# Decode scores of a half batch in three runs of two, two and one feature stages instead of two runs of three and two

## The chip, the core and the metric

The kernel runs on one core of one Trainium2 chip. The engines that matter here are TensorE (PE in the profile; its weight loads are listed as PEld), VectorE (DVE), ScalarE (ACT) and GpSimd (POOL), which issues the indirect DMAs that gather cache pages. The metric is the device time of one execution in microseconds, as the median of several runs.

## What is computed

The reference is one inference step of one layer, for a prompt of 512 tokens and for a decode batch of 8 sequences with 4 new tokens each. Both groups share the weights.

```python
def layer(h, pos, past_ckv, past_kr, past_pos, s0, lb, norm_g, wg, wu, wd, ...):
    h = h + 0.5 * rmsnorm(swiglu(rmsnorm(h, norm_g[0]), wg[0], wu[0], wd[0]), norm_g[1])
    m, c_kv, k_r, s_fin = mixer(rmsnorm(h, norm_g[2]), pos, past_ckv, past_kr, past_pos, s0, lb, ...)
    h = h + rmsnorm(m, norm_g[3])
    h = h + 0.5 * rmsnorm(swiglu(rmsnorm(h, norm_g[4]), wg[1], wu[1], wd[1]), norm_g[5])
```

The part that the change touches is the decode attention inside `mixer`. For each sequence, 16 queries (4 tokens times 4 heads) attend to 4096 past positions. A past position has a latent row of 256 numbers and a rotary key of 64 numbers, both found through a page table:

```python
s = (jnp.einsum('bqhr,bsr->bhqs', ql, c_kv) + jnp.einsum('bqhd,bsd->bhqs', qr, k_rope)).astype(jnp.float32) * scale
p = jax.nn.softmax(s, axis=-1).astype(c_kv.dtype)
return jnp.einsum('bhqs,bsr->bqhr', p, c_kv)
```

## The kernel before, in words

**The stretch of the program.** After the attention of the prompt the kernel enters a scope called `dec`. There two generators are advanced in turn: `decode()` does the decode attention, and `gb` is the second feed-forward block for the first half of the tokens (256 columns). Each call of `next` on `decode()` is one step; after it `gb` is advanced about once. `gb` is the generator `ffn` with `fine=True`; its matrix multiplications are recorded on lines L259, L277 and L288, with weights split into a high and a low part on ScalarE (L250, `wh`) and VectorE (L251, `wl`).

**Halves.** The past of each of the 8 sequences is cut in two halves of 2048 positions, so there are 16 objects `Half`. Each half goes through these parts:

- `gather` fetches two blocks of latent rows (`craw`, 1 MB each, L1352) and `gather_r` two blocks of rotary keys (`rraw`, L1359), as indirect DMAs that GpSimd issues. A `craw` block sits in one of seven slots (`ulb`, `uhb`, `ha`, `hb`, `mb`, `q0`, `dx`; the profile prints `q0` as `q`). `rraw` has two buffers, so the next `gather_r` waits until VectorE has transposed the current one.
- `turn(st)` transposes 64 of the 320 features of the half (two instructions of 128x512 on VectorE, L1367) into a tile `kh`. There are five such feature stages; stage 0 holds the rotary keys, stages 1 to 4 the latent. `kh` has four buffers (`KHB = 4`), so a fifth `turn` waits until the scores have read the first.
- `score(st)` multiplies a stage's `kh` by the queries: 16 fp32 products of 64 rows by 32 columns over 128 positions, on L1379. The profile counts each of them as two MATMULs with a weight load each, so a stage is 32 MATMULs and a half is 160. The last stage copies the scores out of PSUM (L1385) and takes a maximum (L1387, `mxh`).
- `peak` turns the scores into probabilities: one small product `pm` (L1391), a maximum (L1393), the exponential (L1397), a transpose to `pt` (L1399) and 16 small copies into `pbuf` (L1403), 12 of them on ScalarE and 4 on VectorE.
- `value` multiplies the probabilities by `craw` (32 MATMULs for the two blocks, L1412). When a block has been read, the next `craw` gather may go into its slot. `gathered` (L1420, L1421) collects a sequence once both halves are done.

**What sets the order.** `decode()` runs over `n` and, within it, over five steps `st`. In each step it first scores the stages that the table `RUNS` names for this step, for half `n - 2`; then it may run `peak` (step 1) and `value` (step 4) for half `n - 3`; then it makes one `turn`. So the scores of one half are two bursts of MATMULs within a sequence of feed-forward matrix products: stages 0, 1, 2 in step 2 and stages 3, 4 in step 4, the second directly ahead of `value`. The layer that records the instructions may still move an instruction ahead of others of its engine where its inputs are there.

```python
RUNS = {2: (0, 1, 2), 4: (3, 4)}
```

Of the kernel before, what the change touches and what calls it, by code (L numbers as in the profile page):

```python
# [64 lines left out]
JS = ((8, 9), (0, 1), (2, 3), (4, 5), (6, 7))  # L65
KHB = 4
PEAK = 1
RUNS = {2: (0, 1, 2), 4: (3, 4)}
LEVELS = (32, 16, 8, 4, 2, 1)
CH = 64  # L70

# [39 lines left out]
def hybrid_step_kernel(  # L111
# [443 lines left out]
    with scope("ffn0") as pool:  # L555
# [143 lines left out]
        if True:  # L699
            if True:  # L700
                sst.close()
                st = stg.enter_context(tc.tile_pool(name="st", bufs=1, side="right", reuse_waits="tile"))
# [585 lines left out]
    with scope("dec"):  # L1288
# [134 lines left out]
        def decode():  # L1423
            H = [Half(n) for n in range(NH2)]
            blocks = [h_ for h_ in H for _ in range(2)]
            ups = [(h_, st) for h_ in H for st in range(len(JS))]

            def gather(n=1):
                for h_ in blocks[:n]:
                    h_.gather()  # L1430
                del blocks[:n]

            def turn():
                if ups:
                    h_, st = ups.pop(0)
                    h_.turn(st)
                    if st == 0 and h_.n + 1 < NH2:
                        H[h_.n + 1].gather_r()

            for n in range(NH2 + 4):  # L1440

                def at(k):
                    return H[n - k] if 0 <= n - k < NH2 else None

                for st in range(len(JS)):
                    if at(2):
                        for k in RUNS.get(st, ()):
                            at(2).score(k)
                    if n < 3 and st == 0:
                        if n == 0:  # L1450
                            H[0].gather_r()
                        gather(2 + n // 2)
                    if st == PEAK and at(3):
                        at(3).peak()
                    if st == 1 and at(4) and at(4).i:
                        at(4).gathered()
                    if st == len(JS) - 1 and at(3):
                        for c in range(2):
                            at(3).value(at(4), c)
                            gather()  # L1460
                    if n > 1 or n == 1 and st >= 1:
                        if n != 2 or st >= 2:
                            turn()
                    yield

        def decode_end():
# [33 lines left out]
            nc.vector.tensor_copy(oT[1][:, NH:, HS[1] - TS :], o[:, :P].rearrange("p (h t) -> p h t", h=NH))  # L1500

        ga, gn = decode(), decode_new()
        na, ib = len(JS) * (NH2 + 2) + 4, 0
        for ia in range(na):
# [190 lines left out]
```

## Time and profile before

| | us |
|---|---|
| median of 3 runs | 1250.42 (1248.77 to 1251.25) |
| profiled execution | 1257.12 |
| its span, first to last instruction | 1255.3 |
| PE busy | 1225.7 (98%) |
| DVE busy | 983.8 (78%) |
| ACT busy | 742.0 (59%) |
| POOL busy | 72.4 (6%) |

The decode scores (L1379) run from 716.2 to 953.2 us of the span. The granted TensorE clock is 0.995 over the span. A row of a timeline gives the start in us, the duration in us, the engine, the line, the operation with its output and inputs, the count of merged instructions, and in brackets the idle time ahead of it with what ended it ("issue": the engine waited for nothing that the profile shows). A row of stretches gives the stretch, its length, and the busy time of PE, PEld, DVE, ACT and POOL with instruction counts, then the granted clock, the DMA share and GB/s.

### The profile page before, as it was taken

What the parts mean: (1) busy time and instruction counts of PE and PEld (TensorE: products, weight loads), DVE (VectorE), ACT (ScalarE), POOL (GpSimd) and SP (SyncE); (2) the same over time, 40 slices, a digit from 0 to 9 for tenths busy, and PEclk for the clock granted to TensorE, in tenths of its full rate; (3) what the DMA queues carried; (4) which work ended last, traced back from release to release, by engine and by line L of the source; (5) the groups of instructions that cost most, each with busy time, mean ns of one, the idle gap of its engine ahead of it and who ended that gap; (6) DMA issues with size and microseconds to landing.
All of it is one profiled execution on the core that took longest, in us unless ns stands there. A gap on an engine that the chain in (4) does not pass through costs nothing.

```text
span 1255.3 us, 30001 instructions
## 1 busy us (share of the span) xinstructions
PE 1225.7 (98%) x12366; PEld 1157.1 (92%) x12366; DVE 983.8 (78%) x1976; ACT 742.0 (59%) x1559; POOL 72.4 (6%) x80
## 2 busy tenths in 40 slices
PE   8999999999999999999999899999999999999997
PEld 7999999999999988988889889878888999999997
DVE  7897788878679887877876899989987878466665
ACT  7675545544466655446668656665656777554454
POOL 0000000000000000000000412222310000000000
PEclk9999999999999999999999899999999999999999
DMA  6232333322164122324223959778776635645551
GB/s 236 85 118 87 100 101 101 94 96 94 51 227 158 60 89 69 104 77 148 75 92 118 374 178 347 292 249 299 252 273 218 204 104 191 188 137 182 145 160 59
DMA packets 73113, 195.59 MB, mean 156 GB/s; under 512 B 12336, under 2 KB 27728, under 8 KB 68240
## 3 DMA queue, kind: packets, MB, share of 16 engines
q1 hardware_dynamic: 64512, 150.47, 37.0%
q0 software_dynamic: 7168, 41.95, 9.2%
q8 instruction: 97, 1.59, 0.5%
q10 hardware_dynamic: 1296, 1.26, 0.3%
q14 instruction: 40, 0.33, 0.1%
HBM read 183.97 MB, written 9.67 MB: 154 GB/s over the span
## 4 chain that ended last, share of the span: by engine, by line
PE 86%; ACT 6%; DVE 5%; issue 2%; DMA 1%; SPq 0%; DVEq 0%; ACTq 0%
PE acc L259 29%; PE acc L277 18%; PE dn L259 8%; PE Y L561 6%; PE X L561 4%; PE Z L561 4%; PE s L1379 3%; PE acc L717 3%; PE o L1412 2%; ACT wh L250 1%; DVE wl L251 1%; PE pa L938 1%; ACT pbuf L1403 1%; PE acc L288 1%; PE zx L826 1%
## 5 line engine op out<-in xcount | busy, mean ns | idle before, releaser
L250 ACT CAST wh<-wraw 128x1024 fp32r<-128x1024 f32 (+2 forms) x194 | 185.3, 959 | 169.3 <-PE acc L259 108.6
L251 DVE TENSOR_TENSOR wl<-wraw,wh 128x1024 fp32r<-128x1024 f32 (+2 forms) x194 | 214.3, 1107 | 68.6 <-ACT wh L250 67.5
L277 PE MATMUL acc<-uha,wh 128*128 128x256 f32 (+1 forms) x528 | 155.7, 296 | 0.8 <-ACT uha L207 0.8
L277 PE MATMUL acc<-uha,wl 128*128 128x256 f32 (+1 forms) x528 | 150.6, 286 | 0.5 <-DVE wl L251 0.4
L277 PE MATMUL acc<-ula,wh 128*128 128x256 f32 (+1 forms) x528 | 150.9, 286 | 0.0
L259 PE MATMUL acc<-uhb,wh 128*128 128x288 f32 (+1 forms) x432 | 128.0, 296 | 0.0
L259 PE MATMUL acc<-uhb,wl 128*128 128x288 f32 (+1 forms) x432 | 127.0, 295 | 0.9 <-DVE wl L251 0.7
L259 PE MATMUL acc<-ulb,wh 128*128 128x288 f32 (+1 forms) x432 | 127.5, 295 | 0.0
L277 PEld LDWEIGHTS acc<-uha,wh 128*128 128x128 f32 x528 | 99.6, 189 | 8.8 <-issue 7.3
L277 PEld LDWEIGHTS acc<-uha,wl 128*128 128x128 f32 x528 | 99.5, 189 | 2.4 <-DVE wl L251 1.4
L277 PEld LDWEIGHTS acc<-ula,wh 128*128 128x128 f32 x528 | 99.8, 189 | 1.5 <-issue 1.2
L259 PEld LDWEIGHTS acc<-uhb,wl 128*128 128x128 f32 x432 | 81.2, 188 | 1.5 <-DVE wl L251 1.5
L259 PEld LDWEIGHTS acc<-uhb,wh 128*128 128x128 f32 x432 | 81.0, 188 | 0.2 <-ACT uhb L170 0.2
L259 PEld LDWEIGHTS acc<-ulb,wh 128*128 128x128 f32 x432 | 81.1, 188 | 0.1
L259 PE MATMUL dn<-hh,dh 128*128 128x272 f32 x256 | 74.3, 290 | 0.0
L259 PE MATMUL dn<-hh,dl 128*128 128x272 f32 x256 | 73.8, 288 | 0.0
L259 PE MATMUL dn<-hl,dh 128*128 128x272 f32 x256 | 73.6, 287 | 0.0
L1379 PE MATMUL s<-kh,q 64*32 64x128 f32 x2560 | 53.5, 273 | 5.3 <-issue 5.3
L277 PE MATMUL acc<-uhb,wh 128*128 128x272 f32 x176 | 52.8, 300 | 0.0
L1379 PEld LDWEIGHTS s<-kh,q 64*32 64x32 f32 x2560 | 38.5, 105 | 15.4 <-issue 10.5
L259 PE MATMUL acc<-hlb,wh 128*128 128x288 f32 x176 | 52.1, 298 | 0.0
L259 PE MATMUL acc<-hhb,wh 128*128 128x288 f32 x176 | 51.8, 298 | 0.0
(632 smaller groups left out, 3899.0 us busy)
## 6 DMA issues: line engine op xcount, KB each, us to landing
wraw<-w_u SPq DMA_DIRECT2D x66, 512.0 KB
wraw<-w_g SPq DMA_DIRECT2D x65, 512.0 KB
wraw<-w_d SPq DMA_DIRECT2D x40, 384.0 KB
wraw<-w_in SPq DMA_DIRECT2D x24, 512.0 KB
wraw<-w_d SPq DMA_DIRECT2D x32, 320.0 KB
wraw<-w_d SPq DMA_DIRECT2D x16, 512.0 KB
wraw<-w_o SPq DMA_DIRECT2D x16, 512.0 KB
g_S<-state SPq DMA_DIRECT2D x4, 512.0 KB
```

Source lines behind the costliest of these rows:

```text
L250: nc.scalar.copy(wh[:, :kt], w[:, :kt])
L251: nc.vector.tensor_tensor(wl[:, :kt], w[:, :kt], f32(wh[:, :kt]), op=ALU.subtract)
L259: nc.tensor.matmul(out, a, b, start=n == 0, stop=n == last)
L277: nc.tensor.matmul(acc[:, :n], a[:, k], b[:, k], start=k + i == 0, stop=k == kt - 1 and i == 2)
L288: nc.tensor.matmul(acc, a[:, k], b[:, k], start=k + i == 0, stop=k == kt - 1 and i == 2)
L561: nc.tensor.matmul(bank, a[p][:, k], b[q][:, k], start=first and k + n == 0, stop=k == 3 and n == 2, skip_group_check=True)
L717: nc.tensor.matmul(accs[x, d], wts[d][p][:, k], hs[k // 2][q][:, k % 2, x], start=k + n == 0, stop=k == nf - 1 and n == 2)
L826: nc.tensor.matmul(z, w[a][:, k], U[1][b][:, k], start=k + n == 0, stop=k == KD - 1 and n == 2)
L938: nc.tensor.matmul(po[es, c].rearrange("p (n m) -> p n m", m=m), kx[:, cs], up(qx[:, cs], m), start=True, stop=True, skip_group_check=True)
L1379: nc.tensor.matmul(self.s[r][c * 32 : c * 32 + 32, :P], q[rs, j], kh, start=st + jj == 0, stop=st == len(JS) - 1 and jj == 1, skip_group_c ...
L1403: (nc.scalar.copy if g else nc.vector.tensor_copy)(self.p[g * 32 : g * 32 + 32, c // 2, c % 2 * 4 : c % 2 * 4 + 4, self.i * 16 : self.i * ...
L1412: nc.tensor.matmul(o[g : g + 32, :R], self.p[:, c, a], self.craw[c][:, a], start=i + c == 0 and a < 4, stop=i + c == 2 and a >= 4, skip_gr ...
```

## The change

The table that says which stages are scored in which step has three entries instead of two, the first already in step 0, and the transposes of the first two halves are no longer held back for two steps at `n == 2`, so that they are there for the earlier scores. From then on each `turn` belongs to a step that lies two steps earlier against the half's own scores.

```diff
-RUNS = {2: (0, 1, 2), 4: (3, 4)}
+RUNS = {0: (0, 1), 2: (2, 3), 4: (4,)}
@@ decode(), the end of each step
                     if n > 1 or n == 1 and st >= 1:
-                        if n != 2 or st >= 2:
-                            turn()
+                        turn()
                     yield
```

No instruction is added or taken away; they stand in another order. On TensorE, in the half that follows the value product on `ulb` and `uhb` (L288 and L259 are feed-forward products, `s<-kh` the scores, `o<-` the value products; a row counts products, of which the profile shows each score product as two MATMULs; the line with @@ stands for rows that did not change):

```order
 L288 MATMUL acc<-hla,wh 128x256
 L288 MATMUL acc<-hha,wl 128x256
-L1379 MATMUL s<-kh,q_8159 32x128 x32
+L1379 MATMUL s<-kh,q_8159 32x128 x16
 L1412 MATMUL o<-ha,pbuf 32x256 x8
 L1412 MATMUL o<-hb,pbuf 32x256 x8
@@ -5182,4 +5185,5 @@
 L259 MATMUL acc<-hla,wh 128x256
 L259 MATMUL acc<-hha,wl 128x256
+L1379 MATMUL s<-kh,q_8159 32x128 x32
 L259 MATMUL acc<-hha,wh 128x256
 L259 MATMUL acc<-hla,wh 128x256
```

Ahead of the value products there are now 16 score products instead of 32, and a run of 32 stands in the feed-forward products behind them; the run in the middle goes from 48 to 32. Over the whole program the scores stood in 37 unbroken rows and now stand in 52.

On VectorE, behind the split of a feed-forward activation (L171) that the trace of before has at 826.10 us. Before (`pm` and `pt` belong to `peak`, `kh<-rraw` is the transpose of the rotary keys that the next `gather_r` waits for):

```order
L171 TENSOR_TENSOR hla<-sil,hha 128x256
L1393 TENSOR_REDUCE q_8159<-pm 128x16
L1421 COPY q_8787<-o 128x4x16
L1396 SCALAR_TENSOR_TENSOR mq,mbd<-q_8159 128x16
L350 TENSOR_TENSOR sil<-acc,rna 128x256
L1399 STREAM_TRANSPOSE pt<-q_8159 128x256
L1403 COPY pbuf<-pt 32x4x16 x4
L1367 STREAM_TRANSPOSE kh<-ulb 128x512
L1367 STREAM_TRANSPOSE kh<-uhb 128x512
L1367 STREAM_TRANSPOSE kh<-rraw 128x512 x2
```

And with the change:

```order
L171 TENSOR_TENSOR hla<-sil,hha 128x256
L1367 STREAM_TRANSPOSE kh<-ulb 128x512
L1367 STREAM_TRANSPOSE kh<-uhb 128x512
L1367 STREAM_TRANSPOSE kh<-rraw 128x512
L1393 TENSOR_REDUCE q_8159<-pm 128x16
L1421 COPY q_8787<-o 128x4x16
L1396 SCALAR_TENSOR_TENSOR mq,mbd<-q_8159 128x16
L1367 STREAM_TRANSPOSE kh<-rraw 128x512
L1399 STREAM_TRANSPOSE pt<-q_8159 128x256
L350 TENSOR_TENSOR sil<-acc,rna 128x256
L1403 COPY pbuf<-pt 32x4x16 x4
```

The transposes of the last stage and of the rotary keys have moved ahead of the chain of `peak`; the small operations of `peak` and the copies into `pbuf` stand behind them.

## The prediction, made before the changed kernel ran

> **What bounds the kernel now.** The page's first part was read first, then the table of stretches, one stretch for each half, and last the order in time of the engines within a half.
>
> ```profile
> span 1255.3 us, 30001 instructions
> PE 1225.7 (98%) x12366; PEld 1157.1 (92%) x12366; DVE 983.8 (78%) x1976; ACT 742.0 (59%) x1559; POOL 72.4 (6%) x80
> ```
>
> TensorE is busy 98% of the span, so what it does sets the end, and the change moves only TensorE and VectorE work between 711 and 966 us. Below are stretches from the end of one value product to the end of the next, that is one half each (the first row: fourteen halves together).
>
> ```profile
> 748.15:955.37 207.22, 201.26 (x3753) 173.76 (x3753) 187.23 (x412) 125.91 (x335) 47.71 (x49) 1.00 0.79 279
> ...
> 748.15:761.76 13.61, 13.61 (x267) 12.02 (x267) 12.91 (x30) 9.02 (x25) 2.91 (x4) 1.00 0.89 314
> 761.76:777.95 16.19, 16.19 (x289) 14.60 (x289) 15.30 (x30) 10.67 (x28) 4.69 (x6) 1.00 0.95 347
> 777.95:792.28 14.33, 14.33 (x273) 12.73 (x273) 11.96 (x28) 8.53 (x23) 3.35 (x5) 1.00 0.87 328
> 792.28:807.43 15.15, 13.96 (x259) 11.40 (x259) 14.36 (x32) 9.71 (x26) 4.90 (x5) 1.00 0.72 262
> 807.43:821.64 14.21, 13.32 (x255) 10.95 (x255) 13.73 (x33) 8.71 (x25) 4.22 (x5) 1.00 0.81 281
> 821.64:836.44 14.80, 14.50 (x271) 12.63 (x271) 12.06 (x29) 9.24 (x26) 3.79 (x5) 1.00 0.68 226
> 836.44:853.40 16.96, 15.36 (x268) 12.57 (x267) 15.17 (x36) 8.71 (x24) 3.83 (x5) 1.00 0.76 265
> 853.40:869.93 16.53, 16.53 (x289) 14.70 (x289) 14.92 (x31) 9.65 (x23) 3.80 (x5) 1.00 0.88 313
> ...
> 885.00:899.38 14.38, 13.64 (x259) 11.35 (x259) 13.58 (x31) 9.67 (x25) 4.08 (x5) 1.00 0.78 267
> 899.38:913.60 14.22, 13.29 (x255) 10.90 (x255) 13.34 (x33) 8.38 (x25) 4.19 (x5) 1.00 0.75 274
> ```
>
> Two kinds of half are to be seen. In some, PE is busy for the whole stretch (13.61 of 13.61, 14.33 of 14.33) and VectorE has room: TensorE bounds them. In four (from 792.28, 807.43, 885.00 and 899.38) PE has gaps and VectorE is busy for all but 0.79, 0.48, 0.80 and 0.88 us, together 2.95 us: whatever TensorE saves there, VectorE stops it almost at once.
>
> The gaps of PE lie inside the second run of scores. These are rows of PE's timeline in a half with gaps, and in one without:
>
> ```profile
> 802.53 0.89 PE L1379 MATMUL s<-kh,q 64*32 64x128 f32 x42
> 803.59 0.43 PE L1379 MATMUL s<-kh,q 64*32 64x128 f32 x4 [0.17 <-issue]
> 804.34 0.42 PE L1379 MATMUL s<-kh,q 64*32 64x128 f32 x4 [0.32 <-issue]
> 805.06 0.51 PE L1379 MATMUL s<-kh,q 64*32 64x128 f32 x14 [0.29 <-issue]
> 805.49 1.07 PE L1412 MATMUL o<-uhb,pbuf 128*32 128x256 f32 x16
> ...
> 774.92 1.16 PE L1379 MATMUL s<-kh,q 64*32 64x128 f32 x64
> 776.01 1.07 PE L1412 MATMUL o<-mb,pbuf 128*32 128x256 f32 x16
> ```
>
> An undisturbed run of 64 MATMULs takes 776.01 - 774.92 = 1.09 us to the first value product. The disturbed one takes 2.96: the first 42 go at full pace, the rest come in fours. Lost: 1.87 us. The same subtraction for the fifteen runs that a value product follows gives 1.13, 1.87, 2.01, 0.74, 2.11, 0.32, 0.73, 1.72 and 2.03 us in nine and nothing in six, 12.7 us in all. The first and the last of the nine:
>
> ```profile
> 743.99 0.92 PE L1379 MATMUL s<-kh,q 64*32 64x128 f32 x47
> ...
> 746.21 1.07 PE L1412 MATMUL o<-ulb,pbuf 128*32 128x256 f32 x16
> ...
> 908.54 0.92 PE L1379 MATMUL s<-kh,q 64*32 64x128 f32 x44
> ...
> 911.66 1.07 PE L1412 MATMUL o<-uhb,pbuf 128*32 128x256 f32 x16
> ```
>
> What coincides with them is on GpSimd. Its rows for the disturbed run and for the undisturbed one above:
>
> ```profile
> 802.30 0.95 POOL L1359 DMA_INDIRECT rraw<-pool_r,idx  x1 [7.28 <-DVE kh L1367]
> 803.55 0.95 POOL L1359 DMA_INDIRECT rraw<-pool_r,idx  x1 [0.30 <-issue]
> ...
> 772.28 0.95 POOL L1359 DMA_INDIRECT rraw<-pool_r,idx  x1 [7.12 <-DVE kh L1367]
> 773.53 0.95 POOL L1359 DMA_INDIRECT rraw<-pool_r,idx  x1 [0.30 <-issue]
> ```
>
> Where the pair of rotary gathers is being issued during the run (802.30 to 804.50 against 802.53 on), TensorE trickles until about 0.5 us after the pair; where the pair was over before (774.48 against 774.92), it does not. I read it so: while GpSimd issues a pair, new instructions reach TensorE slowly; feed-forward products are slow enough not to notice, a dense run notices after some 44 MATMULs. This is inferred from coincidence.
>
> **The change part by part. First, more runs.** A run of scores costs more than its MATMULs. PE's timeline around a run of 20 and one of 96:
>
> ```profile
> 728.95 0.28 PE L277 MATMUL acc<-ula,wh 128*128 128x256 f32 x1
> 729.16 0.63 PE L1379 MATMUL s<-kh,q 64*32 64x128 f32 x20
> 729.72 0.39 PE L277 MATMUL acc<-uha,wl 128*128 128x256 f32 x1
> 729.95 0.28 PE L277 MATMUL acc<-uha,wh 128*128 128x256 f32 x1
> ...
> 826.48 0.28 PE L277 MATMUL acc<-uha,wl 128*128 128x256 f32 x1
> 826.69 1.59 PE L1379 MATMUL s<-kh,q 64*32 64x128 f32 x96
> 828.21 0.39 PE L277 MATMUL acc<-uha,wh 128*128 128x256 f32 x1
> 828.43 0.28 PE L277 MATMUL acc<-ula,wh 128*128 128x256 f32 x1
> ```
>
> From the last product before a run to the first behind it: 0.77 us with 20 MATMULs, 1.73 with 96, so 12.6 ns for each and 0.52 us without any. Two feed-forward products normally start 0.12 us apart, which leaves 0.40; the second product behind the run comes after 0.22 instead of 0.12, another 0.10. A run costs 0.50 us of TensorE beside its MATMULs. The order has 15 more of them (52 rows instead of 37): +7.5 us. Four of the 15 lie in the four halves where VectorE is the bound and cover them: 2.0 us hidden, +5.5 us on the path. Without that cover it is +7.5.
>
> **Second, the old collisions.** The run directly ahead of the value products is now 32 MATMULs long and ends before the 42 that pass freely; it should not stall, and the gathers are issued elsewhere. In the four halves bound by VectorE 1.87, 2.01, 1.72 and 2.03 us go, but at most its 2.95 us of idle time can come back, of which I take half, 1.5, since its waits on ScalarE stay. In the other halves 1.13, 0.74, 2.11 and 0.73 come back, 4.7 us. (The 0.32 has no gap in the scores; I leave it.) Together -6.2 us, with bounds 0 and -12.7.
>
> **Third, new collisions.** The rotary gathers follow the `rraw` transposes. VectorE's rows at the place that the order shows, and the gather behind them:
>
> ```profile
> 826.44 0.28 DVE L1393 TENSOR_REDUCE q<-pm 128x16 f32<-128x128 f32 x1
> ...
> 828.96 0.71 DVE L1367 STREAM_TRANSPOSE kh<-ulb 128x512 f32<-128x512 f32 x1
> ...
> 831.13 0.95 POOL L1359 DMA_INDIRECT rraw<-pool_r,idx  x1 [7.86 <-DVE kh L1367]
> ```
>
> The chain of `peak` from 826.44 to 828.96 now stands behind the first of these transposes, so the gathers come 2.5 us earlier: 831.13 becomes about 828.6, that is 7.0 us after the end of the value products (821.64). When does a run of 64 stand there? Behind the value products come 12 feed-forward products, a run of 64, 12 more, `pm` and 12 more: 36 x 0.12 + (0.52 + 64 x 0.0126 + 0.10 - 0.24) + about 0.2 = 5.7, so the second run of 64 starts some 6 us after the value products and is through, 0.8 us of MATMULs later, just before the gathers. In the halves with down products there are 18 each time (54 x 0.12): it starts at about 8 us, in the middle of the pair. Three halves are so (from 761.76, 777.95 and 853.40); a stall of 1.7 us as in the like cases above makes 5 us. The first run of 64, 1.6 us after the value products, may also meet the tail of the latent gathers, which I put at nothing, since 44 MATMULs pass freely. Bounds: 0, and some 12 us if the margin of one microsecond in the other halves is gone. I take +5.
>
> What hides nothing: VectorE has the same work and more often a `kh` buffer to wait for that is freed in the same step, but in VectorE's order the copies and splits ahead of it put it some 2 us behind the score that frees it, and I take 0. What is queued behind the moved transposes is the chain of `peak`: `pt` and the copies into `pbuf` come about 2 us later, and the value products wait for them. By the order they are done about 11 us after the value products of the half before, where the next ones start; I take 0, and up to 3 us in all if they are late.
>
> **Sum.** +5.5 - 6.2 + 5 = +4.3 us. The profiled execution, 1257.12 us with a span of 1255.3, would become 1261.4; it lies 6.7 us over the median, and the difference carried to the median of 1250.42 gives 1254.7 us. If the stalls came only with profiling, the runs would still cost their 5.5.
>
> **The rivals.**
>
> - *The collisions simply go.* The margin holds, and in the long halves the gathers miss the run as well: +5.5 - 6.2 = -0.7, 1249.7 us. For it: six of fifteen runs miss the gathers even now. Against it: the run of 64 is now in the middle of the half, towards which the gathers move too.
> - *VectorE is no bound.* Over fourteen halves it is busy 187.23 of 207.22 us, so it could work ahead in the long halves and let the short ones shrink. All 12.4 us of stalls come back and all runs are paid: +7.5 - 12.4 = -4.9, 1245.5 us: faster. It decides if VectorE can be more than one half ahead; the four `kh` buffers speak against it.
> - *The stall belongs to its place and not to the gathers.* No run of 96 stalls, only the run ahead of the value products. Then a run of 32 there is free of it and the other runs too, and the time is 1249.7 as in the first rival. Every disturbed run but the 0.32 overlaps a pair of gathers, which speaks against it. [...]
> - *Collisions in most halves.* The margin of a microsecond is lost; new stalls of 12 us and no more gain on VectorE: +5.5 - 4.7 + 12 = +12.8, 1263 us.
>
> [...]
>
> **How the numbers follow.** My forecast of 1254.7 has a chance of 0.50, its own range is 1251.5 to 1258.5. The collisions go: 0.20. VectorE is no bound: 0.15. The stall belongs to the place: 0.07. Collisions in most halves: 0.08. To hold eight in ten, the range reaches down into the second rival and up to the last: 1246.5 to 1261. A measurement here tells about 0.2%, 2.5 us, from no change. Slower by more: 0.40 of my forecast, the last rival and 0.02 of others, 0.50. Within: 0.10 of the forecast and most of the first and third, 0.31. Faster: the second rival and a little of the first, 0.19.
>
> **What would show it.** In PE's timeline of the changed kernel: runs of 64, 64 and 32 with the 0.22 us behind each of the first two (first term); a run ahead of the value products without gaps of "issue" (second); gaps within the second run of 64 in the halves with down products, beside rotary gathers on POOL (third). VectorE busy to within 1 us in the halves between gate and up products. Wrong would be: PE waits for `pbuf` (L1403) ahead of L1412, or for `kh`; no gaps anywhere; or the stretch from 748 to 955 us shorter than before.

## The result, and the profile after

The changed kernel takes 1258.55 us (median of 6 runs, 1257.11 to 1260.43), the kernel before 1249.63 us (6 runs beside it, 1248.53 to 1251.25). The ratio is 1.0064, with a 95% interval of 1.0054 to 1.0074: the change makes the kernel slower by 8.9 us. The first part of the changed kernel's page (its profiled execution took 1259.84 us):

```profile
span 1258.1 us, 30023 instructions
PE 1227.9 (98%) x12366; PEld 1157.9 (92%) x12366; DVE 984.2 (78%) x1976; ACT 739.1 (59%) x1559; POOL 77.6 (6%) x80
```

Laid beside the trace of before that the prediction read, this explains almost nothing: 1258.1 us of span against 1255.3, a third of the difference between the medians. That execution of before lay 6.7 us over its own median. So the kernel before was profiled once more (the first experiment below; 1251.71 us, span 1249.9), and from here on "before" means that trace. Now the spans differ by 8.2 us, as the medians do.

Where they are is seen in the table of stretches, from the end of one value product to the end of the next. First before (fourteen halves together, then halves 1, 2, 3 and 10):

```profile
746.73:949.45 202.72, 196.51 (x3757) 172.27 (x3753) 186.89 (x412) 125.07 (x335) 52.00 (x49) 1.00 0.80 285
...
746.73:761.29 14.56, 13.89 (x270) 12.09 (x266) 13.86 (x32) 9.00 (x25) 3.32 (x4) 1.00 0.79 296
761.29:777.49 16.20, 16.20 (x293) 14.61 (x289) 14.35 (x28) 10.54 (x27) 4.79 (x6) 1.00 0.94 341
777.49:791.82 14.33, 14.33 (x276) 12.73 (x272) 12.69 (x29) 8.52 (x23) 4.26 (x5) 1.00 0.91 332
...
880.17:893.32 13.15, 12.88 (x262) 11.12 (x258) 12.37 (x29) 8.63 (x23) 4.73 (x5) 1.00 0.80 274
```

The same of the changed kernel:

```profile
747.25:957.79 210.54, 204.34 (x3757) 174.16 (x3753) 187.59 (x411) 125.02 (x337) 52.49 (x49) 0.99 0.76 273
...
747.25:765.53 18.28, 15.88 (x271) 13.01 (x267) 16.44 (x37) 9.64 (x27) 3.97 (x5) 0.91 0.71 252
765.53:782.09 16.56, 16.56 (x292) 14.64 (x288) 12.66 (x24) 10.87 (x28) 4.00 (x5) 1.00 0.80 301
782.09:796.78 14.69, 14.69 (x276) 12.76 (x273) 11.66 (x27) 8.04 (x21) 4.04 (x5) 1.00 0.90 328
...
886.71:900.67 13.96, 13.20 (x263) 11.18 (x259) 13.24 (x30) 8.71 (x24) 3.79 (x5) 1.00 0.73 265
```

The fourteen halves take 210.54 us instead of 202.72. The 7.82 us fall into three parts:

- the first of these halves, in which the new order sets in: 18.28 instead of 14.56, +3.7;
- the six halves in which PE is busy throughout in the trace of before (2, 3, 8, 9, 13, 14; two are shown, 16.20 to 16.56 and 14.33 to 14.69): +2.5 together;
- the seven others, in which PE has gaps in the trace of before: +1.6 together, from +0.81 (13.15 to 13.96) down to -0.15.

What PE waits for between 711 and 966 us has changed too. The table of waits of before, and then that of the changed kernel (engine, line, what it waited for, us in all, times, longest):

```profile
PE pm L1391 <- DVE mxh L1387: 4.4, 7, 1.1
PE acc L288 <- ACT hha L170: 1.1, 1, 1.1
```

```profile
PE acc L288 <- ACT hha L170: 3.4, 2, 2.4
PE s L1379 <- issue: 1.1, 2, 0.6
...
PE s L1379 <- ACT q L1385: 0.4, 2, 0.2
PE s L1379 <- DVE q L1385: 0.3, 1, 0.3
```

Before, PE stands 4.4 us ahead of the small product `pm`, because the maximum `mxh` behind the second run comes late; it does not stand inside any run. With the change that wait is gone, and in its place PE waits for a cast of a feed-forward activation (`hha`), inside or just behind the second run for nothing that this table shows (the last section has the counts), and in the first run for the copies that empty the score tile (L1385).

### The profile page after: what moved, and what is told of

Read it like the earlier page. It is cut to its first block, busy times and chain, and to the rows that moved or that the text cites. A ratio compares the mean times of both kernels' runs of the same rounds, so it can differ in the third digit from the quotient of the medians.

```text
span 1258.1 us, 30023 instructions
## 1 busy us (share of the span) xinstructions
PE 1227.9 (98%) x12366; PEld 1157.9 (92%) x12366; DVE 984.2 (78%) x1976; ACT 739.1 (59%) x1559; POOL 77.6 (6%) x80
## 4 chain that ended last, share of the span: by engine, by line
PE 84%; DVE 7%; ACT 7%; issue 2%; DMA 1%; DVEq 0%; SPq 0%; ACTq 0%
PE acc L259 30%; PE acc L277 16%; PE dn L259 8%; PE Y L561 6%; PE X L561 4%; PE Z L561 4%; PE acc L717 3%; PE s L1379 3%; DVE kh L1367 2%; PE o L1412 2%; ACT wh L250 2%; DVE wl L251 1%; ACT pbuf L1403 1%; PE pa L938 1%; PE zx L826 1%
## 5 line engine op out<-in xcount | busy, mean ns | idle before, releaser
L259 PE MATMUL acc<-uhb,wh 128*128 128x288 f32 (+1 forms) x432 | 128.1, 297 | 0.0
L259 PE MATMUL acc<-uhb,wl 128*128 128x288 f32 (+1 forms) x432 | 127.1, 295 | 1.0 <-DVE wl L251 0.7
L259 PE MATMUL acc<-ulb,wh 128*128 128x288 f32 (+1 forms) x432 | 127.7, 296 | 0.0
L259 PEld LDWEIGHTS acc<-uhb,wl 128*128 128x128 f32 x432 | 81.4, 189 | 1.6 <-DVE wl L251 1.6
L259 PEld LDWEIGHTS acc<-uhb,wh 128*128 128x128 f32 x432 | 81.0, 188 | 0.2 <-ACT uhb L170 0.2
L259 PEld LDWEIGHTS acc<-ulb,wh 128*128 128x128 f32 x432 | 81.1, 188 | 0.1
L259 PE MATMUL dn<-hh,dh 128*128 128x272 f32 x256 | 74.4, 291 | 0.0
L259 PE MATMUL dn<-hh,dl 128*128 128x272 f32 x256 | 73.9, 289 | 0.0
L259 PE MATMUL dn<-hl,dh 128*128 128x272 f32 x256 | 73.7, 288 | 0.0
L259 PE MATMUL acc<-hlb,wh 128*128 128x288 f32 x176 | 52.2, 298 | 0.0
L259 PE MATMUL acc<-hhb,wh 128*128 128x288 f32 x176 | 51.9, 298 | 0.0
L259 PE MATMUL acc<-hhb,wl 128*128 128x288 f32 x176 | 51.5, 295 | 0.0
```

Source lines behind the costliest of these rows:

```text
L259: nc.tensor.matmul(out, a, b, start=n == 0, stop=n == last)
```

## The experiments

In the table, "stretch" is the time from the end of the value products of the first of the sixteen halves to that of the last one in the run's trace, that is the fourteen stretches above and one more of 10 us (before: 212.74 us); "old turns" are the transposes in their old order. It follows the differences of the medians within 1.3 us, in e9_new_from6 within 2.1. The two that fit least are not middling executions: the trace of e5_peak0 is of its slowest of seven, 2.5 us over its median, that of e9_new_from6 of its fastest of five.

| run | what it is | median, us | ratio, 95% | stretch against before, us |
|---|---|---|---|---|
| e0_before | before, again | 1251.71 (one) | | 0 |
| e1_split | runs of 96, 32, 32, old turns | 1252.83 | 1.0015 (1.0006 to 1.0024) | +2.1 |
| e6_size | runs of 64, 64, 32, old turns | 1254.35 | 1.0028 (1.0017 to 1.0040) | +4.0 |
| e7_four | runs of 64, 32, 32, 32, old turns | 1253.66 | 1.0023 (1.0014 to 1.0032) | +3.1 |
| e2_gather | before, rotary gathers two steps later | 1251.38 | 1.0004 (0.9995 to 1.0013) | 0.0 |
| e4_shift1 | two runs, order one step earlier | 1270.08 | 1.0152 (1.0138 to 1.0166) | +18.6 |
| e12_later | two runs, the first one step later | 1266.46 | 1.0121 (1.0106 to 1.0137) | +15.8 |
| e5_peak0 | the change, `peak` a step earlier | 1254.51 | 1.0025 (1.0013 to 1.0036) | +4.9 |
| e8_peak_h1 | the change, `peak` a step later at the start | 1258.23 | 1.0065 (1.0051 to 1.0078) | +7.8 |
| e9_new_from6 | new order from `n` = 6 on | 1255.80 | 1.0047 (1.0033 to 1.0061) | +3.1 |
| e10_new_to6 | new order up to `n` = 6 | 1255.85 | 1.0038 (1.0024 to 1.0052) | +4.6 |
| e11_after | the change, again | 1257.88 | 1.0062 (1.0046 to 1.0077) | +8.5 |

**Are the old collisions there at all?** The kernel before, unchanged (e0_before), and with the call of `gather_r` at another stage (e2_gather):

> The kernel before, once more, for a trace from the same chip as the runs of the changed kernel. If the stalls of the run ahead of the value products (12.7 us in the first trace) belong to every execution, they are found again, 10 to 14 us of them; if they are what made the first profiled execution 6.7 us slower than the median, less than 6 us are left and the span is near 1249 us.

> The kernel before with the rotary gathers issued two transposes later, so that the pair meets no run of scores. If issuing the pair is what stalls the run ahead of the value products, the gaps in it are gone from the trace; if the stalls are in ordinary executions and on the path, it is 3 to 6 us faster, if VectorE takes the place of the stall, within 1 us. If the stall belongs to the place of the run, the gaps stay.

```diff
-                    if st == 0 and h_.n + 1 < NH2:
+                    if st == 2 and h_.n + 1 < NH2:
                         H[h_.n + 1].gather_r()
```

Here is the run ahead of the value products of before that the prediction showed as disturbed, 42 MATMULs and then fours, 2.96 us to the first value product. These are its rows in the new trace, of PE and, for the first of the two gathers, of POOL:

```profile
802.38 1.16 PE L1379 MATMUL s<-kh,q 64*32 64x128 f32 x64
803.46 1.07 PE L1412 MATMUL o<-uhb,pbuf 128*32 128x256 f32 x16
...
802.13 0.95 POOL L1359 DMA_INDIRECT rraw<-pool_r,idx  x1 [7.28 <-DVE kh L1367]
```

The same program and the same place; the gathers begin 0.25 us ahead of the run (in the disturbed case 0.23), and the run takes 1.08 us. All fifteen such runs are undisturbed in this trace (1.08 to 1.21). So a pair of gathers beside a run is not enough to disturb it, and the 12.7 us of stalls belonged to one execution. Moving the gathers made no difference that could be told: there was nothing to gain. That also means that e2_gather says nothing about the cause of the stalls.

**What does the number of runs cost?** Three kernels keep the order of before, with the transposes where they were, and only cut the scores more finely (e1_split, e6_size, e7_four):

> The kernel before with its second run cut in two (96, 32, and 32 MATMULs ahead of the value products); the transposes and the gathers keep their order. Theory of the runs: 15 more runs of 0.50 us on TensorE, 5.5 to 7.5 us slower, less whatever old stalls go. Rival, the order of VectorE makes the change slow (late activations, waits for the copies out of PSUM): that order is not touched here, so 0 us, or faster if stalls go.

> The kernel before, transposes and gathers in their old order, with three runs of 64, 64 and 32 MATMULs as in the changed kernel (in steps 2, 3 and 4). Theory of the runs: 0.37 us for each of 14 more, less the waits that they cover in the halves that VectorE bounds, as in the split of 96, 32 and 32: 2 us slower. If it is the size of the runs that costs, 5 us or more.

> The kernel before with four runs for a half (64, 32, 32, 32), transposes in their old order: 30 more runs. Theory of the runs: another 0.30 to 0.37 us for each run over the split kernel, 4 to 5.5 us, 6 to 8 us slower than before, since the waits that a first extra run covered are used up. If a run costs nothing by itself: 2 us, as the split kernel.

```diff
-RUNS = {2: (0, 1, 2), 4: (3, 4)}
+RUNS = {2: (0, 1, 2), 3: (3,), 4: (4,)}             # e1_split
+RUNS = {2: (0, 1), 3: (2, 3), 4: (4,)}              # e6_size
+RUNS = {1: (0, 1), 2: (2,), 3: (3,), 4: (4,)}       # e7_four
```

Fifteen extra runs cost 1.9 or 3.5 us, thirty cost 2.8 us. The fourteen halves of e7_four, and two of them (3 and 6):

```profile
745.96:951.75 205.79, 204.32 (x3756) 171.02 (x3753) 186.79 (x411) 123.94 (x336) 49.34 (x49) 1.00 0.78 281
...
777.78:792.75 14.97, 14.97 (x276) 12.71 (x273) 13.29 (x29) 8.53 (x23) 4.62 (x5) 1.00 0.83 314
...
819.40:834.12 14.72, 14.72 (x274) 12.46 (x270) 12.38 (x29) 9.68 (x27) 3.32 (x4) 1.00 0.77 263
```

In half 3, which TensorE bounds, two extra runs cost 14.97 - 14.33 = 0.64 us, 0.32 each; in the changed kernel one costs 14.69 - 14.33 = 0.36. In half 6 the kernel with four runs is faster than before (15.40 there), although PE has more to do: it is busy for all of the 14.72. Short runs take PE's idle time ahead of `pm`: its waits for `mxh` go from 4.4 us to 0.9 in e1_split, and in e7_four none is listed. Over fourteen halves the six that TensorE bounds lose 3.9 us, the others together win 0.8. So there is a cover, and it is larger than the prediction said, but most of it is in other halves. Halves 6, 7 and 12 win 0.7, 1.0 and 0.7 us in e7_four; there PE stood 1.1 to 1.2 us ahead of `pm` or of an activation before, and VectorE had 1.7 to 2.0 us of room. The four halves that the prediction named (4, 5, 10 and 11) lose 1.2 us together, with eight extra runs.

The three medians are not the price of the runs alone. In e1_split and e7_four some runs stand still for a while without a releaser (the last section has the counts): PE's waits there are 2.0 us in three runs of e1_split and 0.8 us in one of e7_four. Both e1_split and e7_four came out cheaper than the theory of the runs expected.

**Does the place of the runs against `peak` matter?** Two kernels with two runs, as before, in other steps (e4_shift1, e12_later):

> Two runs as before (96, and 64 ahead of the value products), but the transposes and the first run one step earlier, half of what the change moves. Theory of the runs: no more runs, 0 us, within 2 us either way for stalls. Rival, the order of VectorE makes the change slow: about half of its 8.9 us, 4 us slower.

> The kernel before with two runs, transposes held back one step more and the first run one step later: the opposite of what the change does. If early transposes are what costs at the start, this gives time back, 1 to 3 us faster; if the scores then wait for the last transposes, whose lead is one step shorter, TensorE shows waits for kh and it is slower by 2 us or more.

```diff
-RUNS = {2: (0, 1, 2), 4: (3, 4)}
+RUNS = {1: (0, 1, 2), 4: (3, 4)}                    # e4_shift1; e12_later has 3 for 1
@@ the end of each step
-                        if n != 2 or st >= 2:
+                        if n != 2 or st >= 1:       # e12_later: st >= 3
```

One step earlier costs 19 us, one step later 15.8, with not a single run more, and far more than either was expected to cost. The loss does not grow with the distance either: the change moves the first run two steps and costs 8.9. The tables of waits say on what, the first row of e4_shift1, the other two of e12_later:

```profile
PE o L1412 <- ACT pbuf L1403: 8.4, 8, 1.8
```

```profile
PE pm L1391 <- DVE mxh L1387: 9.9, 7, 3.1
PE s L1379 <- DVE kh L1367: 2.4, 3, 1.4
```

Earlier transposes push the chain of `peak` back until the value products wait for `pbuf`; a later first run makes `mxh` late for `pm`. The old order stands between the two. A step of order is worth several times what fifteen runs are worth.

**How much of the loss is the order of `peak`?** The changed kernel with `peak` called a step earlier, which was to put its chain ahead of the transposes on VectorE again:

> The changed kernel with the chain from scores to probabilities one step earlier, so that on VectorE it stands ahead of the two moved pairs of transposes again; the three runs stay. Theory: of the 8.9 us the 15 more runs cost 5.5 (0.37 us each, from the lengths of undisturbed halves), and the rest is the order of VectorE and ScalarE, late activations ahead of one product and a waiting chain: 5 to 6 us slower than before. Rival, runs alone: 8 to 9 us slower as the changed kernel. Rival, order alone: no slower than 1 us.

```diff
-PEAK = 1
+PEAK = 0
```

In the trace this is done only in part. In most halves the first step of the chain (L1393) now stands ahead of the rotary transposes, but `pt` and the copies into `pbuf` still stand behind them; half 7 of e5_peak0, VectorE:

```profile
845.25 0.25 DVE L1393 TENSOR_REDUCE q<-pm 128x16 f32<-128x128 f32 x1
845.42 0.69 DVE L1367 STREAM_TRANSPOSE kh<-rraw 128x512 f32<-128x512 f32 x1
...
847.04 0.43 DVE L1399 STREAM_TRANSPOSE pt<-q 128x256 f32<-128x256 f32 x1
```

The loss falls to 3.6 us. In the traces halves 6, 7, 10 and 11 are shorter by 0.54, 0.57, 0.87 and 0.38 us than with the change, and they become as short as with the old order, or shorter; the first half stays long (18.11). In halves 10 and 11 of the changed kernel the second run of 64 was disturbed; here is half 10 of the changed kernel, PE and POOL:

```profile
893.11 1.29 PE L1379 MATMUL s<-kh,q 64*32 64x128 f32 x64
895.16 0.39 PE L277 MATMUL acc<-uha,wh 128*128 128x256 f32 x1 [0.76 <-issue]
...
893.17 0.95 POOL L1359 DMA_INDIRECT rraw<-pool_r,idx  x1 [4.77 <-DVE kh L1367]
894.43 0.95 POOL L1359 DMA_INDIRECT rraw<-pool_r,idx  x1 [0.30 <-DVE sil L352]
```

And the same run of e5_peak0:

```profile
892.71 1.16 PE L1379 MATMUL s<-kh,q 64*32 64x128 f32 x64
893.80 0.39 PE L277 MATMUL acc<-uha,wh 128*128 128x256 f32 x1
...
892.60 0.95 POOL L1359 DMA_INDIRECT rraw<-pool_r,idx  x1 [3.83 <-DVE q L1421]
```

The gathers stand beside the run in both, yet it takes 2.05 us to the next product in one and 1.09 in the other. And a run can be disturbed with no gather near it. In e1_split, PE and the next gather:

```profile
902.14 0.65 PE L1379 MATMUL s<-kh,q 64*32 64x128 f32 x27
903.43 0.41 PE L1379 MATMUL s<-kh,q 64*32 64x128 f32 x5 [0.64 <-issue]
...
903.98 0.95 POOL L1359 DMA_INDIRECT rraw<-pool_r,idx  x1 [8.28 <-DVE kh L1367]
```

From 896 us on GpSimd issues nothing until 903.98, and by then the run is over. So gathers beside a run are not enough to disturb it, and a run can stand still without them. What is read from the counts in the last section is that TensorE has come to the end of a block of its instructions there. In half 10 of the changed kernel such a block ends with the 64th MATMUL of the run. In half 12 the stop of e5_peak0 comes after 62 MATMULs of the run, that of the changed kernel after 59; three later, the block of half 10 would end behind the run, by an estimate from these counts, and PE does not stand there. So the 1.25 us that e5_peak0 gains in halves 10 and 11 cannot simply be put down to the order on VectorE. Whether gathers are needed for the stalls of the trace that the prediction read is not shown: those are of another kind.

**How much of the loss is the start?** The order is switched in the middle, at `n` = 6: the old order first and the new one later (e9_new_from6), or the other way about (e10_new_to6); and the changed kernel is run once more beside them (e11_after):

> The order of before for the first four halves, that of the change from the fifth (n = 6) on, where TensorE is the bound; the two turns are made up there. Theory: the change costs at its start, where it pulls four transposes (2.5 us of VectorE) into a stretch in which VectorE is busy 96% of the time, and the rest is 12 extra runs of which some are covered: about 4 us of the 8.9 go, 4 to 5.5 us slower than before. Rival, the order costs in every half: two thirds of the 8.9 or more stay, 6 to 9 us.

> The reverse: the order of the change for the first halves only, that of before from n = 6 on. Theory of the start: 3.5 to 5 us slower than before although only 3 of the 15 extra runs are made. Rival, a cost in every half: a fifth of the 8.9, 1 to 2 us.

> The changed kernel once more, beside the two above. 8 to 10 us slower than before. If the 2.4 us wait of TensorE for the activation cast in the second half belongs to the change and not to one execution, the stretch between the first and second value product is again 3 us or more longer than the 14.6 us of before.

```diff
-                        for k in RUNS.get(st, ()):
+                        for k in (RUNS6 if n >= 6 else RUNS).get(st, ()):   # e9_new_from6
+                        for k in (RUNS if n >= 6 else RUNS6).get(st, ()):   # e10_new_to6
```

(`RUNS6` is the changed table and `RUNS` the old one; at the switch two turns are added or left out.) In the traces the two parts add up: +3.1 and +4.6 make 7.7, and the change has +7.8. With the old start the first half takes 14.53 us, with the new one 18.21. The medians add up to more than the whole (5.2 and 5.2 against 7.2); with intervals of some 1.8 us to either side on each of them the 3.2 us between are at the edge of what they allow, and the split is no better known than that. In e11_after the first half takes 16.94 us, 2.4 longer than before and not the 3 that were expected (the last section has the reason).

What happens at the new start is seen in VectorE's, ScalarE's and PE's rows of the changed kernel:

```profile
756.65 0.38 DVE L353 TENSOR_TENSOR sil<-sil,acc 128x256 f32<-128x256 f32 x1
...
757.00 3.03 ACT L1403 COPY pbuf<-pt 32x64 f32<-32x64 f32 x12
760.05 0.41 ACT L170 CAST hha<-sil 128x256 fp32r<-128x256 f32 x1
...
760.51 0.51 PE L288 MATMUL acc<-hha,wh 128*128 128x256 f32 x1 [2.40 <-ACT hha L170]
```

and in VectorE's and ScalarE's of before:

```profile
754.02 0.42 DVE L353 TENSOR_TENSOR sil<-sil,acc 128x256 f32<-128x256 f32 x1
...
755.28 0.40 ACT L170 CAST hha<-sil 128x256 fp32r<-128x256 f32 x1
755.70 3.07 ACT L1403 COPY pbuf<-pt 32x64 f32<-32x64 f32 x12
```

The cast that the feed-forward products need stood ahead of the twelve copies, now it stands behind them, and PE waits 2.40 us. Its input `sil` is late too: VectorE ends it (L353) at 757.03 instead of 754.44, behind the transposes that have moved ahead. But with that alone the cast would have been done by 757.5, and PE stands from 758.1 on; what makes the 2.40 us are the copies, begun at 757.00, that stand ahead of the cast on ScalarE. Undoing this at the one place was tried (e8_peak_h1):

> The changed kernel with the chain to probabilities of the second half alone one step later, which puts the cast of the feed-forward activation back ahead of the 12 copies on ScalarE there. Theory: the 2.4 us wait of TensorE for that cast and the 3.4 us at half clock behind it (1.7 us) go: 4 us less than the changed kernel, 4.5 to 5.5 us slower than before. Rival, runs alone: 8 to 9 us slower as before.

```diff
-                    if st == PEAK and at(3):
+                    if st == (2 if n == 4 else PEAK) and at(3):
```

It gains nothing that can be told. The wait for `hha` falls to 0.9, but the table of waits has a new row:

```profile
PE o L1412 <- ACT pbuf L1403: 1.6, 1, 1.6
```

Behind this wait the granted clock falls (its mean from 748 to 766 us is 0.91), as it does behind the 2.40 us of the changed kernel (0.91 there too; the last section), and the half that follows is longer by 0.7 us. VectorE is full ahead of the place (busy 17.87 of the 18 us from 730 on in the changed kernel, before 16.82), so it is likely that any order there makes something late; that is argued, not shown. No kernel tried here beats the kernel before.

## Why the prediction was right, and where not

The forecast was slower by 4.3 us, at 1254.7; measured is slower by 8.9 at 1258.55 (7.2 in the repetition). Direction and the wide range (1246.5 to 1261) hold; the forecast's own range of 1251.5 to 1258.5 is missed by 0.05 us, and the size is about half. Of the four terms of the sum one stands in its kind, one did not exist, one is right in size for a wrong reason, and the one that was put at nothing is the largest.

**More runs: +5.5.** The kind is right, the price was too high: 0.50 us a run was forecast, 0.36 measured in a half that TensorE bounds. The mistake is in the slope. All MATMULs were taken at 12.6 ns, from runs of 20 and 96. Two runs of before, and two of the changed kernel with the product ahead of the first:

```profile
898.62 0.28 PE L277 MATMUL acc<-uha,wl 128*128 128x256 f32 x1
898.83 1.59 PE L1379 MATMUL s<-kh,q 64*32 64x128 f32 x96
900.35 0.39 PE L277 MATMUL acc<-uha,wh 128*128 128x256 f32 x1
```

```profile
902.07 0.28 PE L277 MATMUL acc<-uha,wl 128*128 128x256 f32 x1
902.28 1.16 PE L1379 MATMUL s<-kh,q 64*32 64x128 f32 x64
903.37 0.39 PE L277 MATMUL acc<-uha,wh 128*128 128x256 f32 x1
...
911.63 0.67 PE L1379 MATMUL s<-kh,q 64*32 64x128 f32 x32
912.22 1.07 PE L1412 MATMUL o<-uhb,pbuf 128*32 128x256 f32 x16
```

From product to product a run of 96 takes 1.73 us and one of 64 takes 1.30; ahead of the value products a run of 64 takes 1.08 and one of 32 takes 0.59. The new run of 64 costs 1.30, less the usual 0.12 between products, plus the 0.10 behind it: 1.28. The two others become shorter by 0.43 and 0.49. That leaves 0.36 us, exactly what the halves show. Fifteen times 0.36 is 5.4 us of TensorE; with the old order of turns it comes to 1.9 to 3.5 at the end, since the halves in which PE has gaps hide more than the 2.0 us allowed for them. The rule was sound; its cover was too small, and put in the four halves that VectorE bounds, while most of it lies in halves 6, 7 and 12.

**Old collisions: -6.2.** There was nothing to win. The prediction took the stalls of one execution for a property of the kernel. The warning was on the page: that execution lay 6.7 us over the median, and the sum was moved down to the median as if the 6.7 were spread evenly, while the stalls were most of it: of the 5.4 us between the two traced executions of before, 4.5 lie in the fourteen halves. The sentence that the stalls might come only with profiling named the case without drawing the sum from it.

**New collisions: +5 in the long halves.** In the changed kernel's trace second runs are stretched by 3.6 us in all, but not in the halves with down products: from 767.85, 774.07, 857.46 and 863.67 all runs take 1.09. The large ones lie at 893.11, 906.63 and 920.49 (2.05, 1.96 and 1.94 instead of 1.09), and the repetition has the same three (2.54, 2.21 and 2.19) and a fourth, in a half with down products (1.99 from 770.34). The place is wrong but for that one, and so is the cause: all seven are of the kind that is read in the last section as the end of a block of instructions. That the size agrees is chance. How much of it reaches the end is not settled.

**First run of 64 against the latent gathers: nothing.** Three first runs lost 1.65 us together, two of them (1.2 us) for another reason: a first run now comes so soon behind the last one that the score tile is not yet copied out (the waits for `q`, L1385, above). For the third (0.42 us from 798.39) no releaser shows. So the term was not nothing, and the two waits that show a releaser were not for the gathers.

**The order of `peak`: 0, up to 3.** This is the step that failed. With the same run sizes and the old turns the loss is 3.5 us (e6_size), with `peak` called earlier 3.6 (e5_peak0), with the change 8.9 or 7.2: by the medians the order of the turns and runs is worth 3.6 to 5.4 us. The traces show where in part: the start takes 3.7 us more in the changed kernel, of which 1.7 are longer waiting ahead of the feed-forward product (2.40 us against 0.67) and 1.7 the halved clock behind it. The prediction asked only if the value products would wait for `pbuf`. They do not. But what moves back on VectorE moves back everything behind it, the feed-forward activations too, and at the start of the new order these were what PE waited for (and the copies into `pbuf`, ahead of the cast on ScalarE). The list of what is queued behind the moved transposes named `pt` and `pbuf` and left out L352 and L353, which stand in the same rows. "VectorE within 1 us of the bound" was read as a cover; that it is also why a shift on it is paid for is likely, but not shown. Nor is it shown how much the chain of `peak` itself is worth: e5_peak0 moves only its first step, and part of what it gains is where blocks of instructions end.

**The rivals.** "The collisions simply go" and "VectorE is no bound" rested on gains that did not exist. "The stall belongs to its place" falls too: the run ahead of the value products has none in the ordinary trace, and others have. "Collisions in most halves" comes nearest to the time of the four (1263) and has the mechanism wrong.

**What stays open.** Why eight runs of scores went on in small groups in the one execution that the prediction read; what decides whether the clock is halved behind a wait of some 2 us; and how the loss divides between the start and the rest beyond what two traces and two medians say.

## What to carry to other kernels

Before a stall in a profile is priced as something to be won, hold the profiled execution's time against the median: where it lies over it by more than the change is expected to bring, take a second trace first. Where a second engine is nearly as busy as the one that bounds the stretch (VectorE for 17.87 of 18 us here, PE for 17.86), price a change of order on it by everything that is queued behind the moved work, not only by the chain that the change is about. The price of a burst that is cut in two is the sum of the new piece and of what the old pieces lose, each read from rows of its own length and its own neighbours. And where an engine stops with no releaser, count its instructions: a stop at the same count in execution after execution (here after 64, 63 and 59 MATMULs in both traces of the changed kernel) belongs to the program.

## What the runs showed of the hardware

**Runs that are held up without a releaser.** Two kinds are to be told apart. In the tables of waits of eleven traces other than the one that the prediction read, PE waits 18 times between 711 and 966 us inside or just behind a run of scores with no releaser: 4 times in e11_after, 3 times each in the changed kernel, e1_split and e8_peak_h1, twice in e9_new_from6, once each in e5_peak0, e7_four and e10_new_to6, and not at all in e0_before, e4_shift1 and e12_later. In the changed kernel's trace 18113, 18625 and 19137 TensorE instructions (MATMULs, weight loads and the few semaphore instructions listed) stand ahead of its three stops, which is each time 193 more than a multiple of 256. One row in the profile's table of DMA queues fits to that; it is the same before and with the change (packets, MB, share of 16 engines):

```profile
q8 instruction: 97, 1.59, 0.5%
```

Its packets have 16384 bytes each, and there is one for each 257 of the 24890 TensorE instructions in the trace that the prediction read and the 24913 in that of the changed kernel. In the trace's records of these packets the three stops end 1.34, 1.46 and 1.30 us after a packet has landed. Numbered in order, each packet belongs to one such place, 256 instructions behind the last: of 192, 96 each in the trace that the prediction read and in that of the changed kernel, none is passed sooner than 1.28 us after its packet's landing. It is read here so: TensorE has come to the end of its instructions there and waits for the next block. That is inferred from these counts and times; the profile names no releaser. It would also be why the changed kernel stops after the same 64, 63 and 59 MATMULs in both of its traces, and why small moves of the order can shift or remove such a stop.

The other kind is in the trace that the prediction read alone: eight runs that go on in small groups, most of them fours to sixes, at counts that have nothing in common (the ninth, with 0.32 us, is of the first kind: its place is passed 1.28 us after its packet). All eight lie beside a pair of gathers, but a pair is not enough (2.96 and 1.08 us for the same run in two executions), and the cause stays open.

**The clock after a short wait.** Behind the 2.40 us of waiting at the start of the new order, the granted clock of the changed kernel was:

```profile
760.00:761.00 1.00, 0.49 (x2) 0.26 (x2) 0.51 (x2) 0.43 (x2) 0.00 (x0) 0.81 0.76 266
761.00:762.00 1.00, 1.00 (x6) 1.00 (x5) 1.00 (x2) 0.41 (x1) 0.00 (x0) 0.50 0.51 205
```

It stayed at 0.50 until 764 us, so some 3.4 us went at half speed, about 1.7 us of loss. A slow piece follows waits of 2.34 us in e10_new_to6, 1.70 in e5_peak0 and 1.64 in e8_peak_h1 at this place too; the mean clock from 748 to 766 us is 0.91 in these three traces as in the changed kernel's. In the repetition PE waited 2.37 us and the clock stayed at 1.00; the half is 1.3 us shorter there (16.94 against 18.28). So a wait of 2.40 us was followed by about 1.7 us of loss in one execution, and one of 2.37 us by none in another. The medians hold both cases: of the six executions of the changed kernel the three with a mean clock of 0.992 or 0.993 took 1259.28 to 1260.43 us, the three with 0.995 to 0.997 took 1257.11 to 1257.83. In the four of the repetition time and clock do not go together so. The length of the wait alone does not tell the two cases apart: waits of 1.64 and 1.70 us had a slow piece behind them, one of 2.37 us had none.
